# Background sums tied to the progress of products, gate on TensorE, staged output weights and later transposes in one hybrid encoder layer

## The chip, the cores and the metric

One core of one Trainium2 chip runs the whole layer. The metric is the device time of one execution in microseconds; lower is better. Three timed runs of the kernel before gave 3144.81, 3149.28 and 3150.68 us, median 3149.28.

## The reference, cut to what matters

```python
mod = silu(c) @ w_ada + b_ada                  # per stream: prompt (4096 rows), sample (32 rows)
shift, scale, gate = split(mod, 3)
h = rms_norm(x, g_pre) * (1 + scale) + shift
z, xbc, dt_raw, u, v, gt = split(h @ w_in)     # (1024 x 5648)
xbc = silu(causal_conv(xbc))                   # width 4; gives xs, B, C
y = ssd_scan(xs, softplus(dt_raw + dt_bias), -exp(a_log), B, C, state) + d_skip * xs
ssd_out = y * silu(z)
gmlp_out = silu(gt) * u * (tril(w_s) @ layer_norm(v) + b_s)
mix = concat([ssd_out, gmlp_out]) @ w_out      # (2048 x 1024)
out = x + gate * rms_norm(mix, g_post)
```

All arrays are float32; the conv and scan states are returned too.

## The kernel before

The prompt is cut into NB = 8 **blocks** of 512 rows, numbered 0 to 7. The 32 sample rows ride along in block 3. Every product of a matrix runs in float16 with each operand split into a high and a low part (three products for one, `PARTS`). Blocks 0 to 2 multiply plainly (`plain_step`, `v_plain`); from block 3 on (`FROM = 3`) a scheme with seven products in place of eight (`super_step`, `v_products`) is used, which needs four sums and differences of quarters of each weight tile (`SUMS`).

A block consists of: step k = 0 (B and C), the **output projection of the block before** (`out_proj`, two halves of eight weight tiles), the v product (`v_stage`), and steps k = 1 to 8, which carry the eight head pairs (`pair_x` and what follows) and the eight groups (`group_u`). A plain step is 96 products of 128x512; a weight tile (`wt`, `wm`, four slots of the tag "w") feeds 24 of them.

The order is written as a clock of **ticks**: TensorE's loops call `tick()` after every six products, and `later(lag, f)` queues f for so many ticks on. From that program a scheduler makes each engine's order; it may put an instruction ahead of its tick when its operands and buffers allow. Every engine then runs its list in order, and a transfer is issued by SP's or POOL's list in order.

What the change touches:
- **Sums** (`sums_load` to `sums_split`, L376 to L421): 22 jobs in blocks 1 and 2, queued 16 ticks apart. A job loads 2 x 512 KB of weights into spare planes of the rows' region (`spare(prompt.h)`, unused while products are plain), scales them (ACT L396, DVE L397), makes four combinations (DVE L402, L403, L409, L414), splits each (ACT L273, POOL L274) and stores it (POOL L421).
- **Output weights** (`o_tile`, L482; `mtile`, L454): in block 1 the 16 tiles are made: a load `wf` into a "w" slot, the high part by ACT (L462), the low part by DVE (L463), and a store for the later blocks.
- **Gate** (`gate_step`, L1447): in block 1's output projection, tiles k2 = 4 to 11 each take one 512 KB piece of `w_ada` through a "w" slot, and DVE accumulates four 128x512 pieces (L1456, L1458); eight products (L1471) sum over the partitions.
- **Pairs**: `pair_x` does the convolution on DVE (L799, L802) and SiLU on ACT (L789); `pair_xt` transposes the result on TensorE (L1123) 5 ticks after `pair_x` (12 for pair 1); `pair_xdt`, `pair_state` and `pair_y` hang on it by further lags.
- **Staging of block 0** (`stage_squares`, L332): eight Squares of 512 columns a step with an accumulator; `start_rows` (L1557) brings in block 1's rows, which are transposed (L237) in steps 7 and 8.

## Time and profile before

| | us |
|---|---|
| timed runs, median (lowest to highest) | 3149.28 (3144.81 to 3150.68) |
| profiled execution | 3156.24 |
| its span | 3154.5 |
| TensorE busy in the span | 2866.3 (91%) |
| DVE, ACT, POOL busy | 1734.6, 1521.0, 1309.0 |
| mean granted TensorE clock | 0.962 of full speed |

The profile is of one execution. An engine's busy time counts instructions that compute; a wait is put to the releaser that came last. Ends of matrix products are modelled, so a busy TensorE can still be a slow one; the granted clock tells when (1 is 2.4 GHz, one half 1.2 GHz; a mean lies between).

### The profile page before, as it was taken

How to read it: one execution, taken by the hardware profiler on the slowest of the kernel's cores; microseconds unless marked ns; L12 is line 12 of the kernel's file. 1: busy time of each engine (PE TensorE's matmuls, PEld its weight loads, DVE VectorE, ACT ScalarE, POOL GpSimd, SP SyncE). 2: the span in 40 equal slices, each digit the busy share in tenths (PEclk: the TensorE clock that was granted, in tenths of full speed). 3: DMA queues.
4: the chain of work that ended last, by engine and by line, in shares of the span. 5: the costliest groups of instructions: out<-in, count | busy, mean ns of one | idle time of the engine just before them, and what ended most of it. 6: DMA issues, size and time to landing. Idle time of an engine off the chain costs nothing. (4 is left out here: it accounts for less than half of the span.)

```text
span 3154.5 us, 52782 instructions
## 1 busy us (share of the span) xinstructions
PE 2866.3 (91%) x20090; PEld 1819.5 (58%) x20090; DVE 1734.6 (55%) x3706; ACT 1521.0 (48%) x3260; POOL 1309.0 (41%) x1229
## 2 busy tenths in 40 slices
PE   7988777767899999998999999999999999999987
PEld 2444433333454455646886468855886488747863
DVE  5777788564453433635557265565557365625551
ACT  5688554455433454443654345453545355424530
POOL 3466645566532344222553125432443144303540
PEclk8999888988999999999999999999999999999999
DMA  9665467855442433445565276636564566646652
GB/s 329 214 196 164 150 209 246 285 185 178 150 137 94 153 122 119 133 153 177 161 187 161 83 254 201 218 107 224 189 201 156 175 200 199 202 153 210 203 161 60
DMA packets 264295, 559.96 MB, mean 178 GB/s; under 512 B 27371, under 2 KB 114643, under 8 KB 264041
## 3 DMA queue, kind: packets, MB, share of 16 engines
q1 hardware_dynamic: 242088, 483.56, 48.7%
q0 software_dynamic: 21952, 73.04, 6.2%
q8 instruction: 157, 2.57, 0.3%
q14 instruction: 98, 0.79, 0.1%
HBM read 482.52 MB, written 73.97 MB: 176 GB/s over the span
## 5 line engine op out<-in xcount | busy, mean ns | idle before, releaser
L762 PE MATMUL ps_proj<-hTp,wt 128*128 128x256 f16 x7560 | 874.4, 274 | 13.5 <-DMA wt<-wd 6.1
L762 PEld LDWEIGHTS <-wt 128*128 128x128 f16 x7560 | 738.4, 98 | 105.0 <-issue 9.7
L932 PE MATMUL ps_out<-wm,mix 128*128 128x512 f16 x2880 | 660.8, 387 | 52.4 <-DVE wm L463 18.6
L733 PE MATMUL ps_proj<-hTp,wt 128*128 128x512 f16 x2592 | 602.4, 390 | 11.0 <-DMA wt<-wd 11.0
L932 PEld LDWEIGHTS <-mix 128*128 128x128 f16 x2880 | 283.8, 99 | 391.0 <-issue 64.4
L733 PEld LDWEIGHTS <-wt 128*128 128x128 f16 x2592 | 257.9, 100 | 309.4 <-issue 29.9
L1105 ACT ACTIVATE L<-L,acp 128x128 f32<-128x128 f32 x512 | 166.5, 392 | 135.5 <-DMA L<-acdp 111.5
L802 DVE SCALAR_TENSOR_TENSOR xsT<-xp,cols,xsT 128x512 f32<-128x512 f32 (+1 forms) x216 | 226.2, 1049 | 4.5
L1116 POOL TENSOR_TENSOR L<-L,cb 128x512 f32<-128x512 f32 (+1 forms) x144 | 176.5, 1235 | 108.8 <-ACT L L1110 100.0
L1070 ACT ACTIVATE sq<-mix 128x512 f32<-128x512 f32 (+1 forms) x135 | 78.3, 584 | 283.7 <-POOL mix L1196 197.0
L993 PE MATMUL ps_v<-wm,hTp 128*128 128x512 f16 x840 | 188.2, 383 | 15.6 <-DMA wm<-vd 14.5
L1168 DVE SCALAR_TENSOR_TENSOR hc<-hc,dcp,ps_s 128x64 f32<-128x64 f32 x384 | 79.7, 275 | 204.1 <-PE ps_s L1146 204.0
L274 POOL TENSOR_TENSOR mix<-ms,mix 128x512 f16<-128x512 f32 (+1 forms) x72 | 90.8, 1263 | 237.5 <-ACT mix L273 237.4
L1195 POOL TENSOR_TENSOR mix<-mix,E 128x512 f32<-128x512 f32 x72 | 84.1, 1169 | 242.1 <-DVE E L1191 242.1
L1074 POOL TENSOR_TENSOR acc<-acc,sq 128x512 f32<-128x512 f32 (+1 forms) x126 | 146.2, 1162 | 51.7 <-ACT sq L1070 46.5
L1202 POOL TENSOR_TENSOR mix<-mix,us 128x512 f32<-128x512 f32 x64 | 82.0, 1280 | 174.4 <-ACT us L715 87.6
L274 POOL TENSOR_TENSOR v<-vt,v 128x512 f16<-128x512 f32 (+1 forms) x66 | 83.8, 1297 | 162.5 <-ACT v L273 162.5
L993 PEld LDWEIGHTS <-hTp 128*128 128x128 f16 x840 | 82.6, 99 | 118.8 <-issue 23.2
L274 POOL TENSOR_TENSOR hTp<-ta,hTp 128x512 f16<-128x512 f32 x60 | 74.0, 1234 | 177.1 <-ACT hTp L273 177.0
L1123 PE MATMUL ps_xt<-ident,xsT 128*128 128x128 f32 (+1 forms) x264 | 47.3, 303 | 104.9 <-ACT xsT L789 104.9
L274 POOL TENSOR_TENSOR hTp<-hTp 128x512 f16<-128x512 f32 x88 | 107.4, 1225 | 69.9 <-ACT hTp L273 67.0
L1138 POOL TENSOR_TENSOR xde<-xdt,dep 128x512 f32<-128x512 f32 x64 | 68.1, 1064 | 160.2 <-DVE xdt L1138 153.7
(405 smaller groups left out, 4624.0 us busy)
## 6 DMA issues: line engine op xcount, KB each, us to landing
wt<-wd SPq DMA_DIRECT2D x387, 512.0 KB, 3.8
wm<-od SPq DMA_DIRECT2D x104, 512.0 KB, 3.6
wm<-vd SPq DMA_DIRECT2D x86, 512.0 KB, 4.8
L<-acdp SPq DMA_DIRECT2D x128, 256.0 KB, 4.2
hTp<-in_w_in_dram SPq DMA_DIRECT2D x44, 512.0 KB, 5.3
wd<-wt POOLq DMA_DIRECT2D x36, 512.0 KB, 4.5
wd<-hTp POOLq DMA_DIRECT2D x72, 256.0 KB, 3.4
xa<-in_x_prompt_dram SPq DMA_DIRECT2D x32, 512.0 KB, 6.0
```

Of the source, the lines that this page charges most:

```text
L274: eng.tensor_tensor(lo, src, hi, op=ALU.subtract)
L733: nc.tensor.matmul(ps[pi].rearrange("p (h t) -> p h t", h=2), wt[:, pi, a, q * P:(q + 1) * P], prompt.h[:, 2 * kh:2 * kh + 2, b, q, :], st ...
L762: nc.tensor.matmul(ps, wt[:, pi, a, q * P:(q + 1) * P], prompt.h[:, slot, b, q, :], start=(starts and h == 0 and n == 0), stop=(n == 11), ...
L802: nc.vector.scalar_tensor_tensor(dst, xp[:, k:k + Ts], w(k), dst, op0=ALU.mult, op1=ALU.add)
L932: nc.tensor.matmul(ps[c], x(kk, a, c), w[:, kk, b, :], start=(first and n == 0), stop=(last and n == 5))
L993: nc.tensor.matmul(ps, prompt.h[:, slot, a, q, i * P:(i + 1) * P], wt[q // 2][:, q % 2, b, :], start=(starts and n == 0), stop=(n == 11), ...
L1074: eng.tensor_tensor(st.accb if last else st.acc, st.acc, sq, op=ALU.add)
L1105: nc.scalar.activation(L[:, c, :], L[:, c, :], AF.Relu, scale=-1.0, bias=st.ac[:, c, 2 * j + hh:2 * j + hh + 1])
L1116: nc.gpsimd.tensor_tensor(w.L[hh], w.L[hh], st.cb[j // 4][0:st.Q], op=ALU.mult)
L1168: nc.vector.scalar_tensor_tensor(nh[:, hsl], w.hc[:, c, hsl], st.dc[:, c, 2 * j + hh:2 * j + hh + 1], ps_s[:, c * P + hh * HD:c * P + (hh ...
L1195: nc.gpsimd.tensor_tensor(w.m, w.m, w.E, op=ALU.add)
L1202: nc.gpsimd.tensor_tensor(m, m, w.d[1], op=ALU.mult)
```

## The change

Five things are changed.
1. **Sums**: a tiny ACT copy (`mark`) of one column of the latest evicted product is written into the place to be loaded, so that the load waits until that product has been evicted. The parts of a job lie further apart, and the last one uses the output buffer `w.o`.
2. **Output weights**: `wf` goes into one of three spare places of the rows' region, and the "w" slots hold finished tiles alone.
3. **Gate**: eight loads of `w_ada` into the same spare planes of block 0, in steps 1 to 3, each followed 7 ticks later by two float32 products (128x2 by 128x512) on TensorE, which accumulate in two PSUM banks; the DVE accumulation is gone.
4. **Pairs**: in blocks 0 to 2 `pair_xt` comes 8 ticks after `pair_x` instead of 5.
5. **Block 0**: Squares of 1024 columns in place of two of 512 (all but the last tile), at other lags; block 1's rows are loaded together, the second two tiles into spare planes, with other lags.

```diff
-    def phase_a(st, t0, u, lag_sq, lag, then):
+    def phase_a(st, t0, u, lag_sq, lag, then, places=None):
...
-        xt = [load_x(st, t0 + c * st.Q, st.Q, "xa") for c in cs]
+        xt = [load_x(st, t0 + c * st.Q, st.Q, "xa", places and places[i]) for i, c in enumerate(cs)]
...
     def stage_squares(k):
...
-            for kh in range(2):
-                nc.scalar.activation(tmp2(prompt, "junk").bitcast(BF16)[:, 0:512], w.f[n][kh], AF.Square,
+            for kh, f in enumerate(w.f[n][2:] or w.f[n]):
+                nc.scalar.activation(tmp2(prompt, "junk").bitcast(BF16)[:, 0:f.shape[-1]], f, AF.Square,
...
         for j, dst in enumerate((w.a, w.b)):
+            nc.scalar.activation(dst[:, 0:1], mark[-1], AF.Copy)
...
-        later(5, sums_scale, w)
+        later(4, sums_scale, w)
...
-        later(2, sums_second, w, a11, a21)
+        later(4, sums_second, w, a11, a21)
...
-        later(2, sums_third, w, a11)
-
-    def sums_third(w, a11):
+        later(3, sums_third, w)
+
+    def sums_third(w):
...
-        later(1, sums_split, w, 5, w.t, a11)
+        later(1, sums_split, w, 5, w.t, w.o)
...
     def o_tile(half, k2, first):
         def parts(wt):
-            wf = wslot([P, 2, 512], F32, "wf")
+            i = (half * 8 + k2) % 3
+            wf = spare(prompt.h)[:, i * DM:(i + 1) * DM].rearrange("p (k c) -> p k c", k=2)
...
-                if first and 0 <= k - G0 < KT:
-                    order.append((load_wa, (2, k - G0)))
...
                         nc.scalar.activation(ws[pi].d[j], ps[pi], AF.Identity, scale=scw[:, c:c + 1])
+                        mark.append(ws[pi].d[j][:, 0:1])
...
-        later(lag + 5, pair_xt, st, j, w)
+        later(lag + (8 if st is prompt and st.pl else 5), pair_xt, st, j, w)
...
-                if first and 0 <= half * 8 + k2 - G0 < KT:
-                    gate_step(half * 8 + k2 - G0)
...
-    def gate_step(k):
-        if k == 0:
-            t = [wk.tile([P, 512], F32, tag="zsp", name="gacc", bufs=4) for _ in range(4)]
-            acc.extend((t[0:2], t[2:4]))
-        wa = wget()
...
+    def gate_load(k):
+        wa = spare(prompt.h)[:, k % 3 * DM:(k % 3 + 1) * DM]
+        nc.sync.dma_start(out=wa, in_=w_ada[k * P:(k + 1) * P, 2 * DM:3 * DM])
+        later(7, gate_step, k, wa)
+
+    def gate_step(k, wa):
+        if k == 0:
+            pg.extend(psum("ps_gate") for _ in range(2))
+        mod_rows(2, [k], pg, lambda kt: (wa[:, 0:512], wa[:, 512:1024]))
...
+    def first_rows():
+
+        new_rows(prompt, 1)
+
+        def then(u, xt):
+            for q in range(4):
+                later(2 + 2 * q, phase_a_kt, prompt, xt, u, q)
+
+        phase_a(prompt, T, 0, 3, 7, lambda xt: then(0, xt))
+        f = spare(prompt.hN)
+        phase_a(prompt, T, 1, 6, 14, lambda xt: then(1, xt), [f[:, i * DM:(i + 1) * DM] for i in range(2)])
...
-                later(9, stage_squares, k + 2)
-                later(13, stage_scale, k + 2)
+                later(7, stage_squares, k + 2)
+                later(14, stage_scale, k + 2)
+            if first and k == 1:
+                for i in range(KT):
+                    later(2 + 5 * i, gate_load, i)
             if first and k == 7:
-                later(2, start_rows, b + 1, 0, 1)
-                later(16, start_rows, b + 1, 1, 1)
+                later(2, first_rows)
```

How this moves instructions shows at two places.

**ACT, the end of block 1's output projection** (`hTp<-hTp` is a step of a sums job, L396 its scaling; `o<-ps_out` evicts the projection; `wm<-wf` makes an output weight). Before:

```order
L462 ACTIVATE wm<-wf,go_s 128x2x512
L273 ACTIVATE hTp<-hTp 128x512
L396 ACTIVATE hTp<-hTp,sw 128x1024 x2
L273 ACTIVATE hTp<-hTp 128x512 x3
L462 ACTIVATE wm<-wf,go_s 128x2x512
L273 ACTIVATE hTp<-hTp 128x512 x2
L1387 ACTIVATE o,osp<-ps_out 128x512
L1389 ACTIVATE o<-ps_out 128x512
```

Here the ninth and tenth of 22 jobs stand between the output weights. Now the same place, with L384 the mark and L401 the scaling:

```order
L1389 ACTIVATE o,osp<-ps_out 128x512
L1391 ACTIVATE o<-ps_out 128x512
L1109 ACTIVATE L<-L,acp 128x128 x4
L1114 ACTIVATE L<-L 128x512
L1109 ACTIVATE L<-L,acp 128x128 x5
L1114 ACTIVATE L<-L 128x512
L1109 ACTIVATE L<-L,acp 128x128 x5
L384 ACTIVATE hTp<-o 128x1 x2
L1109 ACTIVATE L<-L,acp 128x128 x2
L1114 ACTIVATE L<-L 128x512 x2
L401 ACTIVATE hTp<-hTp,sw 128x1024
```

The first scaling now stands behind the last eviction of the projection. By evicted products on ACT, the last scaling stood 22 evictions of `ps_proj` into block 1's 36 before; it now stands 20 into block 2's, four evictions (one step) apart in the steps.

**SP, the output weights' loads in block 1** (`xr` are rows for the residual, `wa` the gate's pieces, `hTp<-in_w_in_dram` a sums load). Before:

```order
L485 DMA wf<-in_w_out_dram 128x2x512
L531 DMA wa<-in_w_ada_dram 128x1024
L485 DMA wf<-in_w_out_dram 128x2x512
L382 DMA hTp<-in_w_in_dram 128x2x512 x2
L531 DMA wa<-in_w_ada_dram 128x1024
L485 DMA wf<-in_w_out_dram 128x2x512
L386 DMA hTp<-in_w_in_dram 128x8x128
L531 DMA wa<-in_w_ada_dram 128x1024
```

Now:

```order
L491 DMA hTp<-in_w_out_dram 128x2x512
L1308 DMA xr<-in_x_prompt_dram 128x512
L491 DMA hTp<-in_w_out_dram 128x2x512 x3
L1308 DMA xr<-in_x_prompt_dram 128x512 x2
L491 DMA hTp<-in_w_out_dram 128x2x512 x8
L1100 DMA E<-acdp 64x512 x2
L476 DMA wm<-vd_160 128x2048
```

Sums and gate pieces no longer stand among these loads; the first three of the 16 now stand ahead of block 1's step 0 weights or among them.

## Rows read from the trace of the kernel before

**Rows 1.** busy time by stretch, blocks 0 to 2 and the rest

```profile
core 0: us, PE busy (x) PEld busy (x) DVE busy (x) ACT busy (x) POOL busy (x), PEclk, DMA share, GB/s
...
131.50:397.60 266.10, 218.72 (x1183) 114.16 (x1182) 198.31 (x340) 197.28 (x426) 170.65 (x155) 0.92 0.55 174
397.60:429.50 31.90, 21.64 (x110) 9.91 (x107) 20.49 (x37) 14.54 (x24) 16.36 (x16) 0.87 0.85 271
429.50:578.40 148.90, 114.10 (x521) 50.98 (x522) 124.92 (x161) 78.87 (x128) 80.84 (x87) 0.86 0.68 223
578.40:628.90 50.50, 41.60 (x193) 18.55 (x190) 28.53 (x48) 20.46 (x41) 25.47 (x29) 0.97 0.83 285
628.90:901.50 272.60, 210.08 (x1140) 108.26 (x1141) 125.19 (x216) 131.46 (x233) 159.28 (x149) 0.90 0.52 167
901.50:923.20 21.70, 21.70 (x112) 10.21 (x110) 14.04 (x33) 9.85 (x17) 7.62 (x6) 1.00 0.56 179
923.20:1015.80 92.60, 91.75 (x514) 46.42 (x513) 44.35 (x106) 41.80 (x84) 26.51 (x24) 1.00 0.31 101
1015.80:1057.10 41.30, 41.30 (x194) 18.69 (x192) 17.11 (x41) 12.91 (x31) 8.51 (x8) 1.00 0.59 194
1057.10:1273.10 216.00, 203.84 (x1150) 106.91 (x1149) 85.41 (x184) 102.38 (x202) 89.79 (x75) 0.98 0.37 115
...
1394.00:3154.50 1760.50, 1672.74 (x13654) 1218.45 (x13651) 928.72 (x2118) 775.21 (x1760) 640.01 (x590) 0.98 0.56 178
```

**Rows 2.** TensorE's waits in block 0's steps 1 to 8 (sum, times, longest, us)

```profile
PE ps_xt L1123 <- ACT xsT L789: 23.3, 6, 7.4
PE ps_xT L237 <- DVE xa L217: 15.4, 2, 8.7
```

**Rows 3.** TensorE's waits in block 1's step 0 and output projection

```profile
PE ps_out L932 <- DVE wm L463: 18.6, 8, 4.1
PE ps_out L932 <- ACT wm L462: 16.2, 8, 6.3
PE ps_out L932 <- ACT mix L273: 10.3, 1, 10.3
```

**Rows 4.** TensorE's waits in block 1's steps 1 to 8

```profile
PE ps_xt L1123 <- ACT xsT L789: 58.3, 6, 22.5
PE ps_proj L733 <- DMA wt<-wd: 11.0, 2, 8.0
```

**Rows 5.** TensorE's waits in block 2's steps 1 to 8

```profile
PE ps_xt L1123 <- ACT xsT L789: 12.2, 5, 5.4
```

**Rows 6.** timeline, one weight tile's products (start, us, engine, what)

```profile
688.10 5.34 PE L733 MATMUL ps_proj<-hTp,wt 128*128 128x512 f16 x24
```

**Rows 7.** line L526, float32 products of the modulation (ns min/median/max)

```profile
L526 PE MATMUL ps_mod<-wa,sc_c x64: 591/592/1061, 4.5 to 41.7; 128*2 128x512 f32 x64
```

**Rows 8.** groups by line, output projection of block 1, DVE and ACT

```profile
L1458 DVE SCALAR_TENSOR_TENSOR gacc<-wa,sc_c,gacc 128x512 f32<-128x512 f32 x28 | 26.8, 999 | 3.9 <-DMA wa<-in_w_ada_dram 3.9
L463 DVE SCALAR_TENSOR_TENSOR wm<-wf,go_s,wm 128x1024 f16<-128x1024 f32 x15 | 21.5, 1432 | 7.5 <-ACT wm L462 7.5
...
L273 ACT ACTIVATE hTp<-hTp 128x512 f16<-128x512 f32 x28 | 17.2, 626 | 35.9 <-DVE hTp L402 11.1 <-DVE hTp L414 11.1 <-POOL hTp L274 9.4
L462 ACT ACTIVATE wm<-wf,go_s 128x1024 f16<-128x1024 f32 x14 | 16.0, 1142 | 13.1 <-DMA wf<-in_w_out_dram 10.5 <-DVE gacc L1458 2.5
```

**Rows 9.** the same stretch, POOL

```profile
L274 POOL TENSOR_TENSOR hTp<-hTp 128x512 f16<-128x512 f32 x27 | 35.9, 1340 | 18.0 <-ACT hTp L273 17.0 <-DMA wa<-in_w_ada_dram 0.9
```

**Rows 10.** DVE instructions of one shape (ns min/median/max): sums, and a copy

```profile
L409 DVE TENSOR_TENSOR hTp<-hTp x10: 674/692/1523, 629.3 to 820.0; 128x512 f32<-128x512 f32 x10
...
L1157 DVE COPY hc<-Hp x64: 207/218/4900, 114.6 to 3012.1; 128x128 f32<-128x128 f32 x64
```

**Rows 11.** SP's holds ahead of the sums loads (ns), and weights' landing (us)

```profile
L386 SPq EVENT_SEMAPHORE  x46: 17/28/11381, 358.4 to 807.3; - x46
...
wt<-wd SPq DMA_DIRECT2D x387, 512.0 KB, 3.8
```

More of the change, by code (lines that the diff above doesn't have):

```diff
@@ L316, in stage_load @@
             tiles = [tiles[:, n * DM:(n + 1) * DM] for n in range(3)]
-        w.f = [(t[:, 0:512], t[:, 512:1024]) for t in tiles]
+        w.f = [(t[:, 0:512], t[:, 512:1024], t) for t in tiles]
         if k == NSS - 1:
@@ L333, in stage_squares @@
         w.ss = small([P, 2, 4], "wsq")
+        w.split = len(w.f[3]) == 2
         for n in range(4):
-            for kh in range(2):
-                nc.scalar.activation(tmp2(prompt, "junk").bitcast(BF16)[:, 0:512], w.f[n][kh], AF.Square,
+            for kh, f in enumerate(w.f[n][2:] or w.f[n]):
+                nc.scalar.activation(tmp2(prompt, "junk").bitcast(BF16)[:, 0:f.shape[-1]], f, AF.Square,
                                      accum_out=w.ss[:, kh, n:n + 1])
@@ L341, in stage_scale @@
         s, inv = sw[:, 4 * k:4 * k + 4], scw[:, 4 * k:4 * k + 4]
-        nc.vector.tensor_tensor(w.ss[:, 0], w.ss[:, 0], w.ss[:, 1], op=ALU.add)
+        if w.split:
+            nc.vector.tensor_tensor(w.ss[:, 0, 3:4], w.ss[:, 0, 3:4], w.ss[:, 1, 3:4], op=ALU.add)
         pow2_of_ssq(ssq_total(w.ss[:, 0]), [P, 4], "wp4", s, inv)
@@ L372, in hybrid_step_kernel @@
             [("w", k, pi) for k in range(1, NSS) for pi in range(2)])
+    mark = []
     def sums_load(kind, k, i):
@@ L491, in hybrid_step_kernel @@
     order, ready = [], []
-    G0 = 4
     def plan():
@@ L965, in v_plain @@
                 nc.scalar.activation(prompt.v[c][:, j * 512:(j + 1) * 512], ps[c], AF.Identity, scale=sc_v[:, j:j + 1])
+                mark.append(prompt.v[c][:, j * 512:j * 512 + 1])
     def v_stage(active, plain):
@@ L1362, in out_proj @@
                 residual_rows(prompt)
-                for st in active if not first else ():
+                for st in active:
                     st.gp = gate_row(st)
@@ L1389, in out_proj @@
                     nc.scalar.activation(osl, ps[st][c][0:st.Q], AF.Copy)
+                    if st is prompt:
+                        mark.append(osl[:, 0:1])
             if half == 0:
@@ L1396, in out_proj @@
             Q, n, nm = st.Q, st.nch, st.name
-            if first:
-                st.gp = gate_row(st)
             t = small([P, n], "nt" + nm)[0:Q]
@@ L1438, in hybrid_step_kernel @@
     gvc = const.tile([P, KT], F32, name="gvc")
-    sel = const.tile([P, 2, 2], F32, name="sel")
-    nc.vector.memset(sel, 0.0)
-    for s in range(2):
-        nc.vector.memset(sel[:, s, s:s + 1], 1.0)
-    acc = []
-    def gate_step(k):
-        if k == 0:
-            t = [wk.tile([P, 512], F32, tag="zsp", name="gacc", bufs=4) for _ in range(4)]
-            acc.extend((t[0:2], t[2:4]))
-        wa = wget()
-        for s in range(2):
-            for half in range(2):
-                a, c = acc[s][half], sc_c[:, k, s:s + 1]
-                if k == 0:
-                    nc.vector.tensor_scalar(a, wa[half], c, None, op0=ALU.mult)
-                else:
-                    nc.vector.scalar_tensor_tensor(a, wa[half], c, a, op0=ALU.mult, op1=ALU.add)
-        if k == KT - 1:
-            gr, ba, gpo = [wslot([P, DM], F32, nm) for nm in ("gr", "ba", "gpo")]
-            nc.sync.dma_start(out=ba[0:2], in_=io["b_ada"][:, 2 * DM:3 * DM].to_broadcast([2, DM]))
-            nc.sync.dma_start(out=gpo[0:2], in_=io["g_post"].to_broadcast([2, DM]))
-            later(4, gate_rows, gr, ba, gpo)
@@ L1465, in gate_rows @@
-    def gate_rows(gr, ba, gpo):
-        for half in range(2):
-            hsl = slice(half * 512, (half + 1) * 512)
-            ps = psum("ps_gate")
-            for s in range(2):
-                nc.tensor.matmul(ps[0:2], sel[:, s, :], acc[s][half], start=(s == 0), stop=(s == 1))
-            nc.vector.tensor_tensor(gr[0:2, hsl], ps[0:2], ba[0:2, hsl], op=ALU.add)
+    pg = []
+    def gate_load(k):
+        wa = spare(prompt.h)[:, k % 3 * DM:(k % 3 + 1) * DM]
+        nc.sync.dma_start(out=wa, in_=w_ada[k * P:(k + 1) * P, 2 * DM:3 * DM])
+        later(7, gate_step, k, wa)
@@ new lines, in gate_step, with gate_rows @@
+    def gate_step(k, wa):
+        if k == 0:
+            pg.extend(psum("ps_gate") for _ in range(2))
+        mod_rows(2, [k], pg, lambda kt: (wa[:, 0:512], wa[:, 512:1024]))
+        if k == KT - 1:
+            gate_rows()
+    def gate_rows():
+        gr, ba, gpo = [spare(prompt.h)[:, i * DM:(i + 1) * DM] for i in range(3)]
+        for half in range(2):
+            nc.vector.tensor_copy(gr[0:2, half * 512:(half + 1) * 512], pg[half][0:2])
+        nc.sync.dma_start(out=ba[0:2], in_=io["b_ada"][:, 2 * DM:3 * DM].to_broadcast([2, DM]))
+        nc.sync.dma_start(out=gpo[0:2], in_=io["g_post"].to_broadcast([2, DM]))
+        later(4, gate_sum, gr, ba, gpo)
@@ L1473, in gate_rows, with gate_sum @@
+    def gate_sum(gr, ba, gpo):
+        nc.vector.tensor_tensor(gr[0:2], gr[0:2], ba[0:2], op=ALU.add)
         nc.vector.tensor_mul(gr[0:2], gr[0:2], gpo[0:2])
@@ L1565, in then @@
             for q in range(4):
-                later((1 if b == 1 else 8) + (2 if b == 1 else 6) * q, phase_a_kt, prompt, xt, u, q)
+                later(8 + 6 * q, phase_a_kt, prompt, xt, u, q)
         phase_a(prompt, b * T, u, lag, lag + 4, then)
+    def first_rows():
[6 more added lines that the diff above has]
+        phase_a(prompt, T, 1, 6, 14, lambda xt: then(1, xt), [f[:, i * DM:(i + 1) * DM] for i in range(2)])
     for b in range(NB):
```

4 lines of the change are left out of this document (2 added, 2 removed).

## The prediction

> **What bounds the kernel now.** I read the busy time by stretch first. Its columns give the length, each engine's busy time and the granted clock [rows 1]. TensorE is the bound: from 1394 us on, where block 3 and the later ones run, it is busy 1672.7 of 1760.5 us. The change touches nothing there, since block 3 on keeps the old lag and all sums are made by then; I carry those 1760.5 us over as they are.
>
> Blocks 0, 1 and 2 do the same plain products, so block 2 is a twin by which the others are measured. Steps 1 to 8 take 266.1 us in block 0, 272.6 in block 1 and 216.0 in block 2. Step 0 with the gap behind it takes 31.9 in block 1 and 21.7 in block 2, the output projection 148.9 and 92.6, the v product with its gap 50.5 and 41.3 [rows 1]. Block 2 has none of the sums and makes no weights. The excess is 50.1 + 56.6 + 10.2 + 56.3 + 9.2 = 182.4 us, and that is the ground on which this change can win.
>
> Next come TensorE's waits, which say what ends its idle time. In block 0's steps the transposes of a pair wait for ACT's SiLU six times, 23.3 us, and the transposes of block 1's rows wait twice, 15.4 us [rows 2]. In the output projection every idle microsecond is a wait for a weight in the making (18.6 by DVE, 16.2 by ACT), and 10.3 us pass before its first product [rows 3]. In block 1's steps the pair's transposes wait 58.3 us, the longest time 22.5, and one weight tile comes late [rows 4]. Block 2 has the same lags and waits 12.2 us [rows 5]. So block 1 loses its time to a backlog on ACT and DVE, which are in order, more than to the lag.
>
> The backlog is the sums. In block 1's output projection ACT does 28 of their splits, which cost it 17.2 us of work but 35.9 us of standing still in front of them, for DVE or POOL to finish the step before [rows 8]. Behind each such stand wait evictions, SiLUs and output weights.
>
> **The change part by part.** The sum is made against the profiled execution, 3156.2 us (span 3154.5 and 1.7 around it); it stands 7.0 above the median of the three runs, well inside my range.
>
> *Pairs.* Three ticks are 18 products, and 24 take 5.34 us [rows 6]: 4.0 us more for DVE's convolution and ACT's SiLU. Of block 0's six waits the longest keeps 3.4 of its 7.4, the others average 3.2 and go: **-19**. What is late next is `pair_y`, moved as far, and `E`, held three ticks longer in a ring of five buffers; with one pair per 16 ticks I cost both at nothing, hidden while ACT and DVE are busy 74% of block 0's steps, and at the 4 us of one wait each if they fill up.
>
> *Block 1's rows.* The first pair of tiles gets three ticks more, the second is loaded some ten ticks earlier. Of 15.4 us I take half: **-8**, between 0 and -15. SP issues as many loads; the two into the region that held staged weights must wait for the last conversion of step 7, and behind them stand only small loads.
>
> *Gate.* Sixteen float32 products come into block 0's steps. Those of the modulation at the start take 592 ns each [rows 7]: **+9.5**, all on TensorE's path. The Trainium skill, "FP8 and Floating Point Precision", TensorE Precision Notes, says true FP32 takes four passes through the array. By that and 222 ns for 512 columns (5.34/24) a product would take an estimated 0.89 us and sixteen 14.2 us, 4.7 us more than my term; the row, whose end is modelled, decides for me. Eight loads of 512 KB enter SP's queue in block 0, where DMA is busy 0.55 of the time, and as many leave block 1, where it is 0.68 [rows 1]. The larger Squares only relieve ACT, which is off the path.
>
> *Step 0 of block 1.* Its 10.3 us end with a split behind an output weight whose load was issued late. Three such loads now go ahead, and the sums among them are gone: **-6**, between 0 and -10.
>
> *Output projection.* DVE loses 28 + 4 accumulations of 1.0 us, some 32 us of its 124.9 busy, and the sums [rows 8]. A weight costs ACT 1.14 and DVE 1.43 us against 5.34 us of products, so neither is a bound by its work. What held them up was the shared ring: two slots per tile, the gate's pieces between, DVE behind `gacc`. With finished tiles alone in four slots and `wf` three deep I leave 6 of the 34.8 us idle: -29. The eight gate products go, 8 x 0.59: -4. TensorE is also 22.3 us busier than in block 2 for the same products, at a granted clock of 0.86 against 1.00 [rows 1], that is, partly at 1.2 GHz after waits; 18 of it is clock, and I give back 14. Together **-47**; the bounds are -20 (only the DVE-ended waits go) and -56.
>
> *v product.* The late tile's 8.0 us [rows 4] stood behind sums loads on SP: **-7**, between 0 and -9.
>
> *Steps 1 to 8 of block 1.* Idle is 62.5 us, 12.2 in block 2. The sums are still here, but one job per 16 ticks, each step of it at a tick where the step before should be done. I leave the twin's 12.2 and 6 more: -44, and half of the 6.2 us of low clock: **-47**. The bounds are the lag alone (six waits, at most 4.0 each, so some -21) and -56.
>
> *Block 2.* Thirteen jobs come in. A job is four POOL subtractions of 1.34 us [rows 9], four splits on ACT, five short operations on DVE; at one per 24 us POOL and ACT have room (busy 89.8 and 102.4 of 216.0). The marks put SP behind ACT, and behind a waiting load stand weight tiles; three of them are ahead. The lag takes back up to 8 of 12.2 us, and I charge 12 for new waits: **+4**, between -10 and +12 on this path.
>
> Sum: -19 - 8 + 9.5 - 6 - 47 - 7 - 47 + 4 = -120.5, so 3156.2 - 120.5 = **3036**. The bounds: all excess gone gives about 2972; the direct effects alone (-19 + 9.5 in block 0, -20, -21, +12) give 3117.
>
> **The rivals.**
> - *The staging stays a bound.* If the chain load, ACT, DVE still ends half of the waits, the projection gives 22 in place of 47: 3061. For it speaks that each weight still needs three engines in turn; against it that DMA ended only 10.5 us of ACT's waits there [rows 8].
> - *The sums take their price along.* Block 1's extra idle of 50 us for some nine jobs is 5.6 us a job. If that is the job's own price and not the crowd's, block 1's steps win only 2 and block 2 pays 13 x 5.6 = 73 less 8: 3036 + 45 + 61 = 3142. For it speaks that a DVE copy of one shape takes from 207 to 4900 ns, so something does stretch DVE; against it that a sums operation in block 1 has a median of 692 and at most 1523 [rows 10]. The Trainium skill, "SBUF — State Buffer", SBUF: two separate sides, names what it would be: DVE and GpSimd (POOL) share a port pair as an exclusive lock, held for a whole instruction. By that rule the 13 x 4 subtractions could each hold DVE up in block 2; no row here shows what POOL did during the long copies.
> - *Block 0 pays.* Two of eight PSUM banks are held for 35 ticks and 4 MB more are loaded; if TensorE waits for a bank or a piece, block 0 comes out 15 us worse instead of 17.5 better: 3069. No wait for a bank is among block 0's waits now.
> - *Slower: the marks block SP.* A sums load now waits for ACT to pass the mark, and the weight tiles queued behind it wait too. Three tiles ahead are 16 us of cover less 3.8 us to land [rows 11], so it decides once SP is held over some 12 us. SP was held up to 11.4 us before such a load already [rows 11], and a late tile has cost 8.0 us. At that price 22 jobs cost 176 us, block 1's steps and v product win nothing: 3036 + 54 + 176 = 3266. Against it: a mark is the last eviction, which ACT has done when it gets there.
> - *The change doesn't do what it says*, the sums are still run ahead: the orders of ACT and SP speak against it. About 3110.
>
> **How the numbers follow.** My forecast has 0.64; the staging rival 0.12, the sums' price 0.07, block 0's 0.10, SP's 0.05, sums ahead 0.02. The forecast's own spread is about 2992 to 3075; with staging and block 0 the range goes to 3095. That leaves out SP, the sums' price and the last, 0.14, and a little below. No change is within 0.2%, 6 us, about what a measurement of this kernel can tell. All but SP's case and some of the sums' price lie below: faster 0.93, same 0.02, slower 0.05.
>
> **What would show it.** Right: the projection in block 1 near 102 us at a clock over 0.95, with waits for `wm` under 10 us; steps 1 to 8 near 226 us in block 1 and 249 in block 0; `ps_xt` waiting under 30 us over three blocks; sums scalings one per step until block 2's fifth. Wrong: new waits of TensorE for `wt`, for `ps_gate` or for a bank; SP held before a sums load for over 12 us; block 2's steps over 230 us; or block 0's unchanged, if ACT and DVE, not the lag, set its pace.

## The result and the profile after

The changed kernel takes **3117.9 us** (median of 4 runs, 3111.95 to 3120.18), the kernel before 3149.98 beside it (4 runs, 3144.81 to 3154.27). The ratio is 0.9896, with a 95% interval from 0.9875 to 0.9917: faster by about 1%, or 32 us, where 114 were forecast against the median (120.5 against the profiled execution). The time lies above the range, by 23 us. The profiled execution of the changed kernel took 3111.95 us, span 3110.2, so the spans that the two traces show differ by 44.3; the executions that were profiled stand 6 us above and 6 below their medians.

Busy time by stretch of the changed kernel, in the order of [rows 1] (block 0's steps 1 to 8, block 1's step 0, its output projection, its v product, its steps 1 to 8, and the same four of block 2):

```profile
core 0: us, PE busy (x) PEld busy (x) DVE busy (x) ACT busy (x) POOL busy (x), PEclk, DMA share, GB/s
132.30:402.00 269.70, 232.74 (x1223) 115.14 (x1222) 172.30 (x329) 186.80 (x372) 163.78 (x142) 0.94 0.56 181
402.00:424.00 22.00, 21.22 (x103) 9.54 (x101) 14.13 (x33) 11.31 (x19) 6.71 (x7) 1.00 0.56 179
424.00:522.90 98.90, 94.20 (x513) 46.70 (x514) 52.76 (x90) 55.72 (x93) 31.27 (x31) 0.98 0.50 163
522.90:566.40 43.50, 41.45 (x194) 18.62 (x191) 18.62 (x42) 16.23 (x38) 15.70 (x16) 1.00 0.79 258
566.40:816.60 250.20, 210.03 (x1141) 108.69 (x1142) 136.20 (x212) 137.36 (x251) 153.17 (x143) 0.93 0.54 170
816.60:839.70 23.10, 21.67 (x111) 9.99 (x108) 15.73 (x31) 11.27 (x22) 13.44 (x13) 1.00 0.69 230
839.70:946.60 106.90, 97.98 (x513) 48.47 (x514) 69.71 (x133) 52.31 (x103) 54.79 (x55) 0.94 0.54 170
946.60:996.20 49.60, 41.62 (x193) 18.60 (x192) 18.98 (x44) 21.16 (x49) 17.93 (x19) 0.99 0.67 220
996.20:1238.10 241.90, 211.49 (x1151) 109.31 (x1152) 125.27 (x218) 131.68 (x250) 134.63 (x123) 0.93 0.48 153
```

Block 1's projection came down from 148.9 to 98.9 us, as forecast, and DVE's work in it from 124.9 to 52.8. But block 0's steps did not get shorter (266.1 to 269.7), block 1's only by 22.4, and all of block 2 grew: 92.6 to 106.9, 41.3 to 49.6, 216.0 to 241.9.

TensorE's waits in block 0's, block 1's and block 2's steps 1 to 8, which answer to [rows 2, 4, 5] (sum, times, longest, us):

```profile
PE ps_s L1150 <- POOL xde L1142: 23.0, 7, 8.5
PE ps_xt L1127 <- ACT xsT L792: 11.9, 3, 6.6
...
PE ps_xt L1127 <- ACT xsT L792: 30.5, 6, 17.3
PE ps_s L1150 <- POOL xde L1142: 9.6, 4, 5.7
...
PE ps_xt L1127 <- ACT xsT L792: 23.8, 4, 14.5
PE ps_s L1150 <- POOL xde L1142: 6.6, 3, 4.6
PE ps_proj L735 <- DMA wt<-wd: 6.1, 1, 6.1
```

The chain of a pair runs through these engines: convolution (DVE), SiLU `xsT` (ACT), transposes `ps_xt` (TensorE), `xdt` (DVE), `xde` (POOL), product of states `ps_s` (TensorE), new state `hc` (DVE), output products `ps_y` and `ps_o` (TensorE). In block 0 the wait of the transposes halved and a new one stands right behind it in the chain: `ps_s` waits for POOL's `xde`. Both links together, the 58.3 us of block 1 became 40, the 12.2 of block 2 became 30. Block 1's rows no longer make TensorE wait (15.4 us gone), and what is left of the waits in step 0 and the projection of block 1, the answer to [rows 3], is small:

```profile
PE ps_a L886 <- DVE acp L872: 3.2, 1, 3.2
PE ps_out L935 <- ACT mix L273: 0.8, 1, 0.8
PE ps_out L935 <- DVE mix L274: 0.7, 1, 0.7
```

For the experiments I cut each trace at TensorE's first and last products of a kind: S is all from the end of a block's v product to the next output projection (steps 1 to 8 and the next step 0), O the projection, V the v product. Lengths in us:

| kernel | S0 | O1 | V1 | S1 | O2 | V2 | S2 | from block 3 on |
|---|---|---|---|---|---|---|---|---|
| before | 297.9 | 148.9 | 42.6 | 302.2 | 92.6 | 41.4 | 236.8 | 1843.6 |
| changed | 291.5 | 98.9 | 41.4 | 275.3 | 106.9 | 43.5 | 268.8 | 1834.4 |
| e1, no sums | 293.4 | 98.9 | 41.4 | 220.8 | 92.6 | 41.4 | 223.1 | 1832.0 |
| e2, lag 5 | 284.7 | 98.9 | 41.4 | 298.2 | 106.7 | 41.4 | 283.5 | 1839.2 |
| e3, states later | 284.3 | 97.3 | 41.4 | 266.0 | 107.6 | 41.4 | 261.6 | 1837.6 |
| e4, two gate products | 278.5 | 98.9 | 41.4 | 274.8 | 106.2 | 42.2 | 270.5 | 1834.9 |
| e6, subtractions on DVE | 291.2 | 98.9 | 41.4 | 254.3 | 103.7 | 41.4 | 251.6 | 1833.5 |
| e8, no marks | 292.4 | 108.2 | 65.9 | 303.9 | 92.6 | 41.4 | 223.1 | 1836.1 |
| e11, e3 and e6 | 284.6 | 97.3 | 41.4 | 252.1 | 104.8 | 41.4 | 244.5 | 1833.4 |
| e18, e11 and more lag | 280.8 | 98.8 | 41.4 | 235.0 | 104.8 | 41.4 | 240.0 | 1831.8 |

The last column begins with block 2's output projection and ends with TensorE's last product. It varies by a dozen us among kernels that differ in nothing there; the 9.2 that the change seems to win in it are of that size and are not explained.

### The profile page after: what moved, and what is told of

It is laid out like the page before. It is cut to its first block, busy times and chain, and to the rows that moved or that the text cites. A ratio compares the mean times of both kernels' runs of the same rounds, so it can differ in the third digit from the quotient of the medians.

```text
span 3110.2 us, 52787 instructions
## 1 busy us (share of the span) xinstructions
PE 2869.2 (92%) x20113; PEld 1818.3 (58%) x20114; DVE 1701.9 (55%) x3664; ACT 1531.8 (49%) x3246; POOL 1312.3 (42%) x1229
## 5 line engine op out<-in xcount | busy, mean ns | idle before, releaser
L935 PE MATMUL ps_out<-wm,mix 128*128 128x512 f16 x2880 | 650.5, 384 | 10.7 <-ACT mix L273 6.6
L935 PEld LDWEIGHTS <-mix 128*128 128x128 f16 x2880 | 281.9, 99 | 340.1 <-issue 14.4
L997 PE MATMUL ps_v<-wm,hTp 128*128 128x512 f16 x840 | 186.9, 381 | 16.1 <-DMA wm<-vd 14.9
L935 PE MATMUL ps_v<-wm,hTp 128*128 128x512 f16 x576 | 126.7, 379 | 1.9 <-DMA wm<-vd 1.9
L273 ACT ACTIVATE mix<-ms 128x512 f16<-128x512 f32 (+1 forms) x144 | 82.5, 582 | 85.0 <-DVE ms L1264 84.0
```

The costliest lines, as they stand in the source:

```text
L273: nc.scalar.activation(hi, src, AF.Copy)
L935: nc.tensor.matmul(ps[c], x(kk, a, c), w[:, kk, b, :], start=(first and n == 0), stop=(last and n == 5))
L997: nc.tensor.matmul(ps, prompt.h[:, slot, a, q, i * P:(i + 1) * P], wt[q // 2][:, q % 2, b, :], start=(starts and n == 0), stop=(n == 11), ...
```

## Experiments

All are edits of the changed kernel, timed in three rounds each beside the kernel before, which took 3143.9 to 3151.8 us beside them; so medians of different groups compare to some 0.25%, and where less matters I use the ratio to the kernel before, with its interval (the changed kernel: 0.9896).

### The sums left out, or only loaded (e1, e5)

```diff
-            for n, job in enumerate(jobs[10:]):
-                later(4 + 16 * n, sums_load, *job)
+            pass
...
-            for n, job in enumerate(jobs[:10]):
-                later(4 + 16 * n, sums_load, *job)
+            pass
```

e5 keeps these loops and drops `later(4, sums_scale, w)` at the end of `sums_load`.

> The changed kernel without any of the 22 sums jobs (blocks 3 on read the plain weights in place of the sums, so the output is wrong from block 3). Theory 1, each job has a price for TensorE wherever it stands: block 2 goes back to its time before (out projection 93, v product with its gap 41, steps 1 to 8 216 to 222 us), block 1's steps 1 to 8 come to 222 to 230; in all 65 to 80 us off, about 3040 to 3053. Theory 2, the longer lag of the transposes and the new order of SP's and ACT's work make block 2 slow, the sums little: block 2's steps stay over 235 and the time over 3095.

> The changed kernel with the marks and loads of the 22 sums jobs, but without their scaling, subtractions, splits and stores (blocks 3 on read plain weights in their place, so the output is wrong from block 3). Without the whole jobs it took 2993.6 us, with them 3117.9: 124 us, 5.65 a job. Theory 1, the price is the work on ACT, DVE and POOL between a projection's evictions and a pair's chain: 2994 to 3010. Theory 2, it is the marks, which hold SP and the weight tiles behind a sums load: 3050 or more, with waits of ps_proj for wt.

e1 took 2993.6 us (0.9505, 0.9488 to 0.9522), e5 2998.3 (0.9524, 0.9506 to 0.9542). The sums cost 124 us (123 by the ratios), 5.65 a job on average, more than I had thought even after the result, and some 5 of the 124 are marks, loads and SP. S1, O2 and S2 of e1:

```profile
567.30:788.10 220.80, 219.64 (x1250) 115.33 (x1249) 89.89 (x196) 115.35 (x205) 99.30 (x76) 1.00 0.39 128
788.10:880.70 92.60, 91.75 (x514) 46.40 (x513) 44.34 (x106) 41.75 (x84) 26.50 (x24) 1.00 0.31 101
922.10:1145.30 223.20, 221.00 (x1396) 124.64 (x1394) 94.00 (x216) 120.44 (x230) 100.76 (x80) 1.00 0.42 134
```

TensorE is busy 219.64 of S1's 220.80 us at a granted clock of 1.00: without sums, blocks 1 and 2 with the longer lag have no waits to speak of, and are shorter than the twin by which I measured (S2 before: 236.8). Block 0, where the changed kernel runs no job, stays as long as it was (293.4 against 291.5). The changed kernel's S1 is 54.5 us longer than that of e1: TensorE idles 43.6 us in it against 1.2, and is busy 231.7 us for the same 1250 records, at a granted clock of 0.94. So some 12 of the 54.5 us are products that took longer at the lower clock; the rest is waiting.

### The lag taken back, and the lag carried on (e2, e3)

```diff
-        later(lag + (8 if st is prompt and st.pl else 5), pair_xt, st, j, w)
+        later(lag + 5, pair_xt, st, j, w)
```

```diff
-        later(4, pair_state, st, j, w)
+        later(7 if st is prompt and st.pl else 4, pair_state, st, j, w)
```

> The changed kernel with the transposes of x back at five ticks (everything else as changed). Theory 1, the longer lag only hands the wait on to the product of states behind POOL: the time stays within 6 us of the changed kernel's 3117.9; in block 0's steps ps_xt waits some 20 us again and ps_s under 6, their length 265 to 275. Theory 2, the lag is worth what the prediction gave it: block 0's steps grow by 15 to 19 us, block 1's by some 10; 3140 or more.

> The changed kernel with the product of states seven instead of four ticks behind the transposes (pair_y moves with it). Theory 1, the 23.0 us that ps_s waits for POOL in block 0 are that fixed distance, and with three ticks more most go: block 0's steps 250 to 256, blocks 1 and 2 a few us each; 3090 to 3105. Theory 2, DVE, ACT and POOL are full in block 0 and set its pace, and a wait taken away comes back at another place (ps_y, or ps_xt): block 0's steps stay within 4 us of 269.7, the time within 6 of 3117.9.

e2 took 3147.8 us (0.9990, 0.9977 to 1.0003): the lag is worth 30 us, about as much as the whole change. The first theory for this run fell, and so did the place at which the prediction had put the gain: with five ticks S0 is shorter by 6.8 us, and S1 and S2 are longer by 22.9 and 14.7. In block 0 the lag costs, since the wait passes on to `ps_s`; it pays in blocks 1 and 2. In S2 it pays as much without sums as with them: from 236.8 us in the kernel before to 223.1 in e1, 13.7, no job running there in either. So the sums' price in S2 is the same at both lags, 46.7 us with five ticks (283.5 against 236.8) and 45.7 with eight (268.8 against 223.1); for S1 no run has five ticks without sums. e3 took 3091.0 us (0.9815, 0.9800 to 0.9829): 27 us off by moving the next link of the chain along. Of block 0's 23.0 us of `ps_s` 3.1 are left, but 12.1 come up at the following link, `ps_o`; S0 wins 7.2.

### The gate's products (e4)

```diff
-        mod_rows(2, [k], pg, lambda kt: (wa[:, 0:512], wa[:, 512:1024]))
+        if k == 0:
+            for half in range(2):
+                nc.tensor.matmul(pg[half][0:2], sc_c[:, k, :], wa[:, half * 512:half * 512 + 512], start=True, stop=True)
```

> The changed kernel with two of the sixteen gate products in block 0, all loads and banks as they are (the gate of the modulation is wrong, so the output rows are). Theory 1, the products cost what their 592 ns say, 14 of them 8.3 us, and the rest of the gate's move nothing: block 0's steps 261 to 262, in all 3109 to 3111. Theory 2, they lie in waits that TensorE has anyway: within 3 us of 3117.9. Theory 3, they cost more than themselves, by waits for their loads: 15 us or more off.

3099.2 us (0.9843, 0.9828 to 0.9857), 18.7 under the changed kernel by the medians of different groups. The traces, which I go by, have less: S0 lost 13.0 us for 14 products (12.5 of them busy time), and the whole span 13.6. That is 0.93 us a product, where 0.59 were forecast, and 14.9 for sixteen. The group of these products in S0 of the changed kernel (line, operation, shapes, count, busy us, mean ns) says why:

```profile
L528 PE MATMUL ps_gate<-hTp,sc_c 128*2 128x512 f32 x32 | 16.4, 640 | 0.0
```

There are 32 records for sixteen products. A float32 product of 512 columns leaves two. That could be seen before: [rows 7] counts 64 where the modulation multiplies two parts, eight pieces and two halves, 32 products. The "eight products" of the gate before (L1471) are such records too: its two loops of two make four products.

### Where the subtractions run (e6)

```diff
-        split(o[:, 0:512], o[:, 512:1024], src, nc.gpsimd)
+        split(o[:, 0:512], o[:, 512:1024], src, nc.vector)
```

> The changed kernel with the 88 subtractions of the sums' splits on DVE in place of POOL (POOL keeps their stores). Theory 1, POOL is the engine that is short: it works 166.6 of 273.3 us from block 1's step 1 on and a pair's xde and masks stand behind the sums' subtractions there, or they hold DVE at the port that the two share; block 1's steps with the next step 0 fall from 275.3 to under 255, in all 3085 or less. Theory 2, DVE is short, since a pair's convolution and xdt stand on it: 88 more operations of some 0.7 us on it make the kernel slower, 3130 to 3160.

3072.0 us (0.9766, 0.9746 to 0.9786): 46 us off (41 by the ratios), by moving 88 operations from one busy engine to another. A pair's convolution (two forms) and state copy on DVE, in S1 of the changed kernel, of e1 and of e6 (count, busy us, mean ns):

```profile
L805 DVE SCALAR_TENSOR_TENSOR xsT<-xp,cols,xsT 128x512 f32<-128x512 f32 x24 | 30.1, 1258 | 0.0
L1161 DVE COPY hc<-Hp 128x128 f32<-128x128 f32 x7 | 18.1, 2588 | 0.0
...
L802 DVE TENSOR_SCALAR xsT<-xp,cols 128x512 f32<-128x512 f32 x8 | 7.5, 932 | 0.0
```

```profile
L805 DVE SCALAR_TENSOR_TENSOR xsT<-xp,cols,xsT 128x512 f32<-128x512 f32 x24 | 24.0, 1002 | 0.2
...
L802 DVE TENSOR_SCALAR xsT<-xp,cols 128x512 f32<-128x512 f32 x8 | 5.2, 649 | 25.8 <-ACT xp L743 25.8
...
L1161 DVE COPY hc<-Hp 128x128 f32<-128x128 f32 x7 | 2.6, 376 | 0.0
```

```profile
L805 DVE SCALAR_TENSOR_TENSOR xsT<-xp,cols,xsT 128x512 f32<-128x512 f32 x24 | 24.1, 1006 | 0.0
...
L802 DVE TENSOR_SCALAR xsT<-xp,cols 128x512 f32<-128x512 f32 x8 | 4.3, 544 | 1.8 <-ACT xp L743 1.8
...
L1161 DVE COPY hc<-Hp 128x128 f32<-128x128 f32 x7 | 3.4, 489 | 0.0
```

Beside POOL's subtractions DVE's own operations are longer: the copy seven times. With 34 instructions more in S1, e6's DVE is busy 157.6 us against 153.0, since the others shrank by nearly as much as the 39 new subtractions take, 38.0 us. The timeline of the changed kernel shows one copy (start us, us, engine; ACT and TensorE left out):

```profile
690.68 0.56 POOL L426 DMA_DIRECT2D vd<-hTp  x1 [0.30 <-POOL hTp L274]
690.86 4.11 DVE L1161 COPY hc<-Hp 128x128 f32<-128x128 f32 x1
...
691.27 1.28 POOL L1199 TENSOR_TENSOR mix<-mix,E 128x512 f32<-128x512 f32 x1
...
692.49 1.16 POOL L274 TENSOR_TENSOR hTp<-hTp 128x512 f16<-128x512 f32 x1
...
693.60 1.27 POOL L1200 TENSOR_TENSOR mix<-mix,zs 128x512 f32<-128x512 f32 x1
```

The copy begins while POOL issues a store of the sums, and ends at 694.97, 0.10 us behind the third of three POOL operations that follow without a gap; the one in the middle is the sums' subtraction. Three more copies in S1 stand in the same pattern and take 4.09 to 4.10 us. The Trainium skill, "SBUF — State Buffer", SBUF: two separate sides, says that GpSimd and certain operations of DVE take a shared port pair as an exclusive lock for a whole instruction, and that the side which comes second fully blocks. These four copies agree in that they end only when POOL is through; that a copy waits through three operations is more than the page says. Two copies in S2 do not show the lock: they began 0.50 us behind the recorded start of a POOL operation of 1.84 and 1.85 us, and took 0.22. The profile's spans on POOL are rough, so which side came first is open there.

### Other places and times for the jobs (e7, e8)

```diff
-            for n, job in enumerate(jobs[10:]):
-                later(4 + 16 * n, sums_load, *job)
+            for n, job in enumerate(jobs[9:]):
+                later(6 + 14 * n if n < 5 else 120 + 14 * (n - 5), sums_load, *job)
...
-            for n, job in enumerate(jobs[:10]):
-                later(4 + 16 * n, sums_load, *job)
+            for n, job in enumerate(jobs[:9]):
+                later(40 + 14 * n, sums_load, *job)
```

e8 drops the line with `mark[-1]` from `sums_load`.

> The changed kernel with the same 22 jobs, 14 instead of 16 ticks apart, none of them begun in the v products or within 8 ticks behind them. Theory 1, the longest waits, 17.3 us in block 1 and 14.5 in block 2 of ps_xt right behind the v product, come from two jobs at a place where DVE, ACT and POOL have the v rows' norm to do, and go: blocks 1 and 2 win 12 to 17 us each, 3085 to 3095. Theory 2, a job costs its 5.65 us wherever it stands: 3112 to 3124.

> The changed kernel without the marks, so that a sums job is no longer tied to the last eviction and runs as early as the order of the engines lets it (about ten in block 1's output projection and v product, the rest in its steps, none in block 2). Theory 1, the price goes with the job: block 2 falls back to some 93, 41 and 223 us, but block 1's output projection and v product lose what the staging had won, 30 us or more; in all within 20 us of 3117.9. Theory 2, tying the jobs to the products is worth much: 3145 or more. Theory 3, the tie is what costs, the staging alone makes room for the sums in the projection: 3090 or less.

e7 took 3115.8 us (0.9901, 0.9885 to 0.9916), e8 3119.1 (0.9913, 0.9895 to 0.9932): neither differs from the changed kernel. In e7 the longest wait of `ps_xt` fell from 17.3 to 9.3 us, and block 2's projection grew from 106.9 to 123.1. In e8 block 2 is as short as without sums (357.1 in all, 62 less than in the changed kernel), and block 1 from its projection on is 62 longer (478.0 against 415.6). That is the second theory of e7 and the first of e8: **a job's price goes where the job goes**, and tying the jobs to the products wins nothing. The price is not made of the same waits each time: in e8's block 1, 18.2 us of `ps_v` and 14.4 of `ps_proj` are waits for tiles late from DMA, where the changed kernel waits 10.0 for such tiles in blocks 1 and 2.

### Which link of the pair's chain (e9, e10)

```diff
-            nc.vector.tensor_copy(w.hc[:, 0, :], w.H)
+            nc.scalar.activation(w.hc[:, 0, :], w.H, AF.Copy)
```

```diff
-        pair_times(st, j, nc.gpsimd, w.xde, w.xdt, st.de)
+        pair_times(st, j, nc.vector if st is prompt and st.pl else nc.gpsimd, w.xde, w.xdt, st.de)
```

> The changed kernel with the copy of a pair's old state (hc from H) on ACT in place of DVE, in all blocks. With the sums, 15 such copies in blocks 1 and 2 take DVE 28.7 us (up to 4.1 each, ending with a row of back-to-back POOL operations), without them 6.5. Theory 1, POOL's operations hold DVE's copies up and with them the pair's chain: 3093 to 3108. Theory 2, the copy is not on the path, since the wait that counts is another one: within 6 us of 3117.9, or slower, ACT being in order.

> The changed kernel with xde, POOL's step in a pair's chain between the transposes and the product of states, on DVE in blocks 0 to 2. Theory 1, POOL's queue is the trouble: it stands up to 11.7 us before a sums subtraction for ACT's half of the split, and the xde behind it makes ps_s wait (23.0 us in block 0, 9.6 and 6.6 in 1 and 2): those waits go and the kernel takes 3080 to 3098. Theory 2, DVE is the short engine: 24 more operations of 0.7 us on it move the wait to DVE, and the time stays within 6 us of 3117.9.

3109.1 us (0.9886, 0.9865 to 0.9906) and 3107.3 (0.9880, 0.9857 to 0.9904): neither can be told from the changed kernel by its ratio, and S1 and S2 stayed within 1.4 us of theirs. S0 won 4.0 and 6.5. So the long copies, clear as they are in the trace, do not set TensorE's pace in blocks 1 and 2: on ACT they take 0.3 us each, and S1 is as long as before. The place of `xde` in POOL's queue does not either: in e10 the 39.2 us of waits for POOL's `xde` are gone, and over blocks 0 to 2 `ps_xt` waits 81.6 us in place of 66.2 and `ps_s` 16.3 for DVE. What the 46 us of e6 go through is thereby not shown. The convolution, which feeds `ps_xt` and shrinks in e6 too, is the nearest candidate; POOL's other work in the chain, with POOL 44.6 us less busy in S1, is another. Neither was tried alone.

### Both gains together, and the rest (e11 to e17)

e11 joins the edits of e3 and e6; e12 adds that of e10.

> The product of states three ticks later and the sums' subtractions on DVE, together. Alone they gave 26.9 and 45.9 us. Theory 1, they take away different waits: 3040 to 3052. Theory 2, both shorten the same waits behind POOL: 3062 to 3075.

> The last kernel with xde on DVE too in blocks 0 to 2. Theory 1, what is left is still POOL's queue: another 10 us or more off. Theory 2, DVE now has the sums and the whole pair's chain and is full: no gain, or slower by up to 15.

e11 took 3055.8 us (0.9718, 0.9694 to 0.9742), e12 3054.0 (0.9710, 0.9688 to 0.9733). The gains nearly add up, 62 of 73 us; `xde` on DVE gives nothing. Left over e1 are another 62 us. e13 to e16, on e11's base, go after engines that stand in front of sums steps:

```diff
-        split(o[:, 0:512], o[:, 512:1024], src, nc.vector)
+        nc.vector.tensor_copy(o[:, 0:512], src)
+        nc.vector.tensor_tensor(o[:, 512:1024], src, o[:, 0:512], op=ALU.subtract)
```

```diff
-        later(4, sums_scale, w)
+        later(7, sums_scale, w)
...
-        later(4, sums_second, w, a11, a21)
+        later(3, sums_second, w, a11, a21)
```

```diff
-        nc.scalar.activation(w.a, w.a, AF.Identity, scale=w.s[0])
+        nc.vector.tensor_scalar(w.a, w.a, w.s[0], None, op0=ALU.mult)
```

e13 is the first, e14 the second, e15 both, e16 all three.

> The kernel of e11 (product of states three ticks later, sums' subtractions on DVE; 3055.8 us) with the first half of each sums split, a copy to f16, on DVE too in place of ACT. ACT then neither works on the splits nor stands in front of them (in the changed kernel some 45 us in block 1's steps, for DVE or POOL to finish the step before), while evictions and SiLUs of the pairs stand behind. Theory 1, that standing is most of what a job still costs: block 1's steps with the next step 0 fall from 252.1 to under 238, block 2's from 244.5 to under 236, in all 3025 to 3040. Theory 2, DVE's work is the price, whoever else waits: 88 more copies of some 0.3 to 0.7 us on it, 3050 to 3080.

> The kernel of e11 with the sums' scaling seven instead of four ticks behind their loads (and the second subtraction three instead of four ticks behind the first, so that a job still ends within 16). Theory 1, DVE and ACT stand in front of the scaling until the load has landed (in the changed kernel DVE 31.5 us in block 1's steps, longest 5.2, ACT 9.3), and the pairs' convolutions wait behind: 3030 to 3045. Theory 2, they stand there when they have nothing else to do: within 6 us of 3055.8.

> The edits of e13 and e14 together. Theory 1, standing in front of sums steps is the rest of the price: 3010 to 3030, some 20 to 40 over the kernel without sums. Theory 2, DVE's work is the rest: 3050 or more.

> As e15, with ACT's half of the scaling on DVE too, so that ACT has no sums work but the marks. Theory 1, what ACT still stands for is the load, and it goes: 3 to 10 us below e15. Theory 2, DVE is full by now: slower than e15 by up to 15.

3052.4, 3060.7, 3056.1 and 3055.6 us (0.9698, 0.9726, 0.9717, 0.9711): no difference from e11 in any of them. The standing is there to see (DVE waits for loads before the sums' scaling, ACT for DVE and POOL before a split), but taking it away won nothing, so by these runs an engine that stands there has nothing more urgent behind it. In S1 of e16 ACT is busy 115.9 us and DVE 180.3, in e11 148.0 and 149.2, and the stretch takes 245.7 and 252.1: it hardly matters which of the two has the work.

e17 takes e11's stores away (`nc.gpsimd.dma_start(out=w.dst[s], in_=o)` in `sums_split`).

> The kernel of e11 (3055.8 us) without the 88 stores of the sums, 256 KB each, that POOL issues; all their computing stays (blocks 3 on read plain weights in their place, so the output is wrong from block 3). Theory 1, DVE's and ACT's work on the sums is what is left of the price: within 10 us of 3055.8. Theory 2, it is the stores, which hold POOL some 0.56 us each and take DMA from 0.39 to 0.59: 3030 or less.

3041.9 us (0.9681, 0.9663 to 0.9699), between the two theories; its interval just overlaps that of e11. Of the 14 us only 6 fall in S1, O2 and S2, where the stores run.

### More distance in the whole chain (e18)

```diff
-        later(lag + (8 if st is prompt and st.pl else 5), pair_xt, st, j, w)
+        later(lag + (11 if st is prompt and st.pl else 5), pair_xt, st, j, w)
...
-        later(4, pair_y, st, j, w)
+        later(6 if st is prompt and st.pl else 4, pair_y, st, j, w)
```

> The kernel of e11 with the transposes of x eleven ticks behind the pair's rows and its output product six behind the states (8 and 4 in e11). Theory 1, since moving sums steps between engines no longer helps, what is left are waits of TensorE for the pair's chain at a fixed distance (ps_xt 13.2 and ps_o 13.6 us in block 0, 10.7 and 7.9 in block 1's steps, 12.1 and 5.0 in block 2's), and more distance takes half of them: 3020 to 3040. Theory 2, the chain is late by the work on ACT and DVE, which grows with nothing and shrinks with nothing here: the waits move on, and it is within 8 us of 3055.8.

3028.7 us (0.9635, 0.9620 to 0.9649), **the fastest version that does all the work: 3.65% under the kernel before**, 89 us under the changed one (82 by the ratios). S1 won 17.1 on e11, S2 4.5, S0 3.8. TensorE's waits over blocks 0 to 2 (from S0 to the end of S2) of the changed kernel, then of e11, then of e18:

```profile
PE ps_xt L1127 <- ACT xsT L792: 66.2, 13, 17.3
PE ps_s L1150 <- POOL xde L1142: 39.2, 14, 8.5
```

```profile
PE ps_xt L1127 <- ACT xsT L792: 36.0, 6, 11.0
PE ps_o L1187 <- DVE hc L1172: 23.9, 8, 5.7
...
PE ps_s L1150 <- POOL xde L1142: 5.8, 5, 2.5
```

```profile
PE ps_s L1150 <- POOL xde L1142: 23.6, 8, 10.8
PE ps_xt L1127 <- ACT xsT L792: 15.0, 3, 7.3
...
PE ps_o L1187 <- DVE hc L1172: 4.7, 4, 2.3
```

The three links together wait 105, 66 and 43 us. With five ticks (e2) it was `ps_xt` alone, 132.8 us in 19 waits. As I read it, TensorE meets the chain at places fixed in its order, and what the sums cost is mostly how late the chain is at those places; both ways help, making it less late (e6) or meeting it later (the change, e3, e18). That the later meeting hides the sums' own price is not shown: e3 and e18 were not run without sums, and in S2 the change's lag hid none of it.

## Why the prediction was wrong

The step that failed is the one on the sums: the prediction let their price vanish with the crowd, and charged block 2 next to nothing for the jobs that it was given. By its own terms, against the lengths in the table (forecast, then measured):

- *Output projection*, -47: **-50.0**. Right, with its mechanism. The waits for `wm` are gone, the clock went from 0.86 to 0.98, and DVE's 124.9 us to 52.8. TensorE's idle time fell by 30.1 (29 forecast) and its busy time by 19.9 (18 forecast; the gate's part of it, four products at 0.93 for eight at 0.59, came out by luck). *v product*, -7: from 50.5 to 43.5, -7; but the late tile came back behind block 2's v product, 6.1 us for 8.0. *Step 0 of block 1*, -6: from 31.9 to 22.0, -9.9.
- *Block 0 and step 0 together* (S0: -19 for the pairs, -8 rows, +9.5 gate, -6 step 0, in all -23.5): **-6.4**. Two terms failed. *Pairs*: I costed what is late next at nothing, and named `pair_y` and `E` for it; the next link is `pair_state`, four ticks behind the transposes whatever their lag, and it waited 23.0 us. By e2 the lag costs block 0 6.8 us in place of winning 19. *Gate*: mis-sized, 14.9 for 9.5 (e4), because a product leaves two records and I took the duration of one. The Trainium skill, "FP8 and Floating Point Precision", TensorE Precision Notes, had it by four passes: an estimated 14.2 us. I let the row decide and had misread the row. The remainder, some -28, is better than the -14 of rows and step 0. Step 0 is -9.9 of it, and the 15.4 us of waits for the rows are gone; but the scheduler had also run four of the sums jobs in S0, two of them in block 0's steps, which no term counts, and they left too. No run divides these.
- *Steps 1 to 8 of block 1*, -47, and with the v product -54: V1 and S1 together **-28.1**. *Block 2*, +4: O2, V2 and S2 together **+48.4**. This is the larger part of the miss, 26 and 44 us, and one wrong step: "I leave the twin's 12.2 and 6 more" and "I charge 12 for new waits". I had read block 1's excess as a backlog, made by the crowd in the projection, that spacing the jobs would dissolve. Counted by their scalings on ACT, the jobs stood before 4 in S0, 6 in O1, 2 in V1 and 10 in S1; now 2 stand in V1, 9 in S1 and 11 from O2 on (13 were forecast). So the crowd in the projection went, while S1 kept all but one of its jobs, and with the lag taken back (e2) it takes 298.2 us against 302.2: the spacing won next to nothing there, and what S1 won is the lag, 22.9 by e2, near the bound of the lag alone (-21). Block 2 pays 62.1 us over e1 for its jobs, where 12 were charged. e7 and e8 show that place and spacing hardly matter: a job costs some 5.65 us where it stands (e1). The rows that I set against that, a sums operation's median of 692 ns [rows 10], say how long a sums operation takes, not how late it makes the pair's chain.
- The rival *"the sums take their price along"* was the right one, at 5.6 us a job and with a chance of 0.07. Its time, 3142, was too high chiefly because it gave the lag nothing in block 1 and 8 in block 2; e2 shows 23 us in S1 and 15 in S2. The row it rested on, a copy of one shape from 207 to 4900 ns, pointed at something real that is not on the path (e9).
- *The marks block SP*: no. SP was held up to 12.1 us before a sums load (below: its waits ahead of these loads in the changed kernel, ns min, median, most, then sum, times and longest in us by what ended them), which answers to [rows 11]. But the 12.1 were not a mark: they ended with the last step of the job before (L419), whose place the load takes; a mark (L384) held SP for 8.6 at most. TensorE's longest wait for a weight tile was 6.1 us, and e5 puts marks and loads at some 5 us in all.

```profile
L391 SPq EVENT_SEMAPHORE  x53: 17/28/12123, 533.7 to 1138.1; - x53
...
SPq L391 <- DVE hTp L419: 54.6, 5, 12.1
SPq L391 <- ACT hTp L384: 49.6, 17, 8.6
```

- *The staging stays a bound*: no. *The sums are still run ahead*: no, they are spread as the diff says, but e8 shows that this alone moves 62 us from block 1 to block 2 and wins nothing.
- The bound of the direct effects alone, 3117, is met by accident: its terms are not the measured ones (-20 for a projection that won 50.0, +12 for a block 2 that lost 48.4). Of the prediction's signs of being wrong, block 2's steps over 230 us (241.9) and block 0's steps unchanged (269.7 for 266.1) came, and so did a hold of SP of over 12 us, though not by a mark.

What stays open: of the 124 us, 41 to 46 go when the subtractions move from POOL to DVE, between 6 and 14 with the stores (on e11), and some 5 are marks and loads. The rest, some 60, lies by exclusion in the computing of the sums on ACT and DVE, the moved subtractions among it; e13 and e16 show that its division between the two does not matter, and no run took it apart further. Whether e6's gain goes through the convolution or through POOL's own queue was not tried.

## What to carry to other kernels

- Before background work is moved from a crowded stretch to a quiet one, take it out altogether in a trial: if the time falls by a fixed price per job, that price moves along with the jobs, and the quiet stretch is quiet only until then.
- A lag at one link of a chain can merely pass the wait on to the next link when that keeps its distance (block 0 here). Move all links, and test the gain block by block.
- Before multiplying a row's duration by a count of instructions, check that row's count against the program: one product can leave two records.

## What the runs showed of the hardware

- DVE's copy of 128x128 float32 took 0.22 us in the median of 64, and 4.11 us when it began beside a store's issue on POOL and three POOL operations followed without a gap. It ended 0.10 us behind the last of them.
- 34 more operations on DVE in S1 raised its busy time by 4.6 us, as the others became shorter while POOL had 40 fewer beside them (e6).
- A float32 product of 128x2 by 128x512 shows two records, 592 ns each in the median, and cost TensorE 0.93 us (e4).
